# The feed-forward of a two-layer decoder trunk, cut into parts of 4, 6, 6 and 6 hidden chunks instead of 6, 8 and 8

## The chip, the core and the metric

The kernel runs on one core of one Trainium2 chip. A core has a matrix engine (TensorE, PE in the profile, with its weight loads shown as PEld), a vector engine (VectorE, DVE), an activation engine (ScalarE, ACT), a general engine (GpSimd, POOL) and a sync engine (SyncE, SP) that here issues nearly all DMAs from HBM. The metric is the device time of one execution in microseconds (us); lower is better. Three executions of the kernel before took 1247.47, 1247.70 and 1248.56 us, so its median is 1247.7 us.

## The reference

The input is a sequence of 512 tokens with 1024 features in float32. Two layers follow each other: the first mixes tokens with a causal convolution module, the second with differential attention. Behind each mixer come a SwiGLU feed-forward and a gated per-layer embedding. The change touches the feed-forward alone:

```python
def swiglu(x, w_gate, w_up, w_down):
    return (jax.nn.silu(x @ w_gate) * (x @ w_up)) @ w_down

        u = rms_norm(h, ffn_norm_g[i])
        h = h + swiglu(u, ffn_w_gate[i], ffn_w_up[i], ffn_w_down[i])
        gate = jax.nn.sigmoid(rms_norm(h, ple_norm_g[i]) @ ple_w_gate[i])
        h = h + gate * (p[i] @ ple_w_proj[i])
```

The hidden width is 2816, which is 22 chunks of 128 rows.

## The kernel before

Everything is held transposed: features on the 128 partitions, the 512 tokens along the free dimension. The stream `h` is eight tiles of 128x512. Each float32 operand of a matmul is split into two parts in the format float32r: `hi` is a cast on ScalarE, `lo` is the operand less `hi`, a subtraction on VectorE. A product then takes three matmuls (`mm3`, lines 166 to 168: lo x hi, hi x hi, hi x lo). Weights are split on the chip as they arrive: `weight` (lines 147 to 162) loads a 128x1024 tile into one of two buffers `wraw` from the SP queue (line 155), casts it (line 159) and subtracts (line 161) into one of four buffers `whi` and `wlo`.

The feed-forward (`ffn`) runs through the hidden chunks in parts, given by `PARTS` as (first chunk, number of chunks): 6, 8 and 8. A part makes its hidden chunks, and then `linear` projects them down and adds the result into `h` (line 881), eight outputs one after the other, the first two together (`group0` is 2). In the last part the new `h` also goes to the next norm.

The chunks of the first part are plain. Gate and up each take 8 x 3 matmuls of 512 columns, lines 869 to 875 scale with the norm's factor `rb`, apply SiLU, multiply, and split the hidden chunk into tiles B0, B1 and so on. `rb` is there only after the first chunk's matmuls. While these chunks run, `Operands.chunk` (lines 664 to 688), called four times behind the plain chunks that `OPS_AT` names, makes the operands of the products that follow.

The chunks of the later parts go in pairs. For a pair, the gate (and the same for up) is a 2x2 block product, done with seven products instead of eight: a `Unit` needs sums of weight blocks (S1 to S4), sums of activation blocks (T1 to T4, from `Operands`), and seven products of 4 x 3 matmuls with 256 columns each. `Unit.load` fetches two weight tiles (line 703; for a gate into A0 and A1, for an up into `wraw`). `Unit.prep` has six steps: 0 splits the blocks A11 and A12, 1 makes S1 and S2 on GpSimd (lines 720 and 721), 2 splits them (for the first unit of a part into four `wk` tiles, lines 726 and 727), 3 makes S3 and S4 on GpSimd (lines 732 and 733), 4 splits S3 (lines 736 and 737), 5 splits S4 and A22. The splits that go through `two` stand at lines 710 and 711. A run over the units of a part prepares each unit while the one before multiplies; the products 4 and 3 of a unit are placed behind the products 1 and 2 of the next one, and those of the last unit stand at the run's end.

The first unit of a part has no unit ahead of it. `HOOKS` places its load and its steps in the projection of the part before: the load at output 5, steps 1 and 3 at output 6, steps 0, 2, 4 and 5 at output 7. This is the order in which the program is written. The order in which each engine and each queue gets its instructions is set by a planner, which simulates the program and puts what is ready first, unless an edge says otherwise: `tc.issue_after(ins)` queues what its block writes for the engine of `ins` behind `ins`. It orders issue on that one engine and waits for nothing.

Of the kernel before, what the change touches and what calls it, by code (L numbers as in the profile page):

```python
# [15 lines left out]
ALU = mybir.AluOpType  # L16
# [7 lines left out]
NC = D // P  # L24
# [2 lines left out]
KW = 31  # L27
DFF = 2816
FC = DFF // P
PARTS = [(0, 6), (6, 8), (14, 8)]  # L30
EPS = 1e-6
LAMBDA_INIT = 0.8 - 0.6 * math.exp(-0.3 * 1)
NEG = -1.0e30
# [44 lines left out]
LT = 2  # L78
LA = 4
PACK = True  # L80
OPS_AT = (1, 2, 4, 5)
HOOKS = {5: (None,), 6: (1, 3), 7: (0, 2, 4, 5)}
HT = S // 2
E1 = True
GLO = 1
QKV = (("q", 0, (0, 0, 0, 0)), ("v", 0, (1, 1, 1, 2)), ("q", 1, (1, 1, 1, 2)), ("q", 2, (1, 1, 2, 1)), ("v", 1, (1, 1, 2, 2)), ("q", 3, (1, 1, 1, 1)))

PROJ1 = 16 + 2 + 8 + 2 * FC + 3 * NC + 8 + 4 * len(QKV)


@with_exitstack
def trunk(ctx, tc, xT, pT, wts, diag, dww, vec, rel, onehot, lamv, out):
# [9 lines left out]
    def sb(shape, tag, bufs, dt=F32):  # L102
        uid[0] += 1
        return pool.tile(shape, dt, tag=tag, name=f"{tag}_{uid[0]}", bufs=bufs)
# [10 lines left out]
    f = lambda ap: ap.bitcast(F32)  # L115
# [27 lines left out]

    wnext = [0]
    loaded = [None]

    def weight(n=1024, pieces=1, between=(), eng=V, after=(None, None), home=None, parts=None, bufs=1):
        i = wnext[0]
        wnext[0] += 1
        raw = sb([P, 1024], *(home or ("wraw", 2)))  # L150
        hi = sb([P, 1024], *((parts[0], bufs) if parts else ("whi", 4)), F32R)
        lo = sb([P, 1024], *((parts[1], bufs) if parts else ("wlo", 4)), F32R)
        for k in range(pieces):
            cut = slice(k * n // pieces, (k + 1) * n // pieces)
            loaded[0] = nc.sync.dma_start(raw[:, cut], wts[i, :, cut])
            if k < len(between):
                between[k]()
            with tc.issue_after(after[1].ins) if after[1] else nullcontext():
                A.copy(hi[:, cut], raw[:, cut])  # L159
            with tc.issue_after(after[0].ins) if after[0] else nullcontext():  # L160
                eng.tensor_tensor(lo[:, cut], raw[:, cut], f(hi[:, cut]), ALU.subtract)  # L161
        return hi, lo

    def mm3(acc, a, b, first, last, **kw):
        (ah, al), (bh, bl) = a, b
        T.matmul(acc, al, bh, start=first, stop=False, **kw)  # L166
        T.matmul(acc, ah, bh, start=False, stop=False, **kw)  # L167
        return T.matmul(acc, ah, bl, start=False, stop=last, **kw)  # L168
# [15 lines left out]
    def wpart(w, k):  # L184
        return tuple(
            t[k // 4][:, (k % 4) * P : (k % 4 + 1) * P] if isinstance(t, list) else t[:, k * P : (k + 1) * P] for t in w
        )
# [99 lines left out]
    def load(c):  # L287
        return lambda: nc.sync.dma_start(h[c], xT[c])

    w0 = weight(pieces=2, between=(load(0),))  # L290
    norm.split(0)
    w1 = weight(pieces=2, between=(load(1), load(2)))
    pair_loads = [loaded[0]]
    pairs = [(w1, w0)]
# [302 lines left out]
    with tc.manual_schedule(engines={V.engine, A.engine}):  # L597
        for c in range(NC + 2):
            if c < NC:
# [3 lines left out]
                hi = A.copy(z[c][0], y[c])  # L603
            if c >= 2:
                lo = V.tensor_tensor(z[c - 2][1], y[c - 2], f(z[c - 2][0]), ALU.subtract)
# [5 lines left out]
    def linear(n_in, src, consume, group0=1, before=None, after=None, split={}, home=None, given={}, at={}):  # L611


        m = 0
        while m < NC:
            g = group0 if m == 0 else 1
            ws = [
                given[m + i] if m + i in given
                else weight(n_in * P, after=split.get(m + i, (None, None)), home=home if m + i == 2 else None)
                for i in range(g)  # L620
            ]
            if m in at:
                at[m]()
            accs = [mm() for _ in range(g)]
            for k in range(n_in):
                if before:
                    before(k)
                for w_, a_ in zip(ws, accs):
                    mm3(a_, wpart(w_, k), src[k], k == 0, k == n_in - 1)
                    if after:  # L630
                        after()
            for i in range(g):
                consume(m + i, accs[i])
            m += g
# [170 lines left out]
    def ffn(norm, after, spare):  # L805
        rb = None
        ops = Operands(norm, spare)

        def units(n, hid):
            us = []  # L810
            for i in range(0, n, 2):
                g, u = Gate(2 * (i // 2), i == 0, "A"), Up(2 * (i // 2) + 1, False, "wraw")
                g.hid = hid
                u.gate, u.at, u.hid = g, i, hid
                us += [g, u]
            for x in us:
                x.b = ops.at
            return us

        def run(us):  # L820
            for n, x in enumerate(us):
                last = us[n - 1] if n else None
                nxt = us[n + 1] if n + 1 < len(us) else None
                x.start()
                if nxt:
                    nxt.load()
                x.p(1)
                if nxt:
                    nxt.prep(0)
                x.p(2)  # L830
                if nxt:
                    nxt.prep(1)
                if last:
                    last.p(4)
                x.p(6)
                if nxt:
                    nxt.prep(2)
                if last:
                    last.p(3)
                x.p(5)  # L840
                if nxt:
                    nxt.prep(3)
                    nxt.prep(4)
                x.p(7)
                if nxt:
                    nxt.prep(5)
            us[-1].p(4)
            us[-1].p(3)

        us = None  # L850
        for at, (f0, n) in enumerate(PARTS):
            if us:
                run(us)
                hid = us[0].hid
            else:
                hid = []
            for i in range(0 if us else n):
                wg, wu = weight(), weight()
                pg, pu = mm(), mm()
                for k in range(NC):  # L860
                    mm3(pg, wpart(wg, k), norm.u[k], k == 0, k == NC - 1)
                if rb is None:
                    norm.diagonal()
                for k in range(NC):
                    mm3(pu, wpart(wu, k), norm.u[k], k == 0, k == NC - 1)
                if rb is None:
                    rb = norm.rows()
                tg, tu = big(), big()
                V.tensor_tensor(tg, pg, rb, ALU.mult)
                A.activation(tg, tg, AF.Silu)  # L870
                V.tensor_tensor(tu, pu, rb, ALU.mult)
                V.tensor_tensor(tu, tu, tg, ALU.mult)
                hl = sb([P, 2, S], f"B{i}", 1, F32R)
                A.copy(hl[:, 0], tu)
                V.tensor_tensor(hl[:, 1], tu, f(hl[:, 0]), ALU.subtract)
                hid.append((hl[:, 0], hl[:, 1]))
                if i in OPS_AT:
                    ops.chunk(OPS_AT.index(i), rb)

            def add(m, acc):  # L880
                V.tensor_tensor(h[m], acc, h[m], ALU.add)
                if at == len(PARTS) - 1:
                    after.chunk(m)

            hooks = {}
            if at < len(PARTS) - 1:
                n2 = PARTS[at + 1][1]
                now = wnext[0]
                wnext[0] += NC
                us = units(n2, [None] * n2)  # L890
                end = wnext[0]
                wnext[0] = now
                x = us[0]
                for m, steps in HOOKS.items():
                    hooks[m] = partial(lambda steps: [x.load() if k is None else x.prep(k) for k in steps], steps)
            linear(n, hid, add, 2, at=hooks)
            if hooks:
                wnext[0] = end
# [281 lines left out]
    for what, at, pace in QKV:  # L1180
        ws = slab(GLO if at > 0 else 0)
        for tb in range(4):
# [12 lines left out]
            elif (what, at, tb) == ("q", 0, 2):  # L1195
                n = wnext[0]
                wnext[0] = PROJ1
                pw = [weight(parts=("B6", "B7"))]
# [6 lines left out]
            elif (what, at, tb) == ("q", 2, 1):  # L1205
                pw.append(weight_in_h(PROJ1 + 1, 0))
            elif (what, at, tb) == ("q", 2, 2):
                w_o1 = weight_in_h(PROJ1 + 3, 4)
            elif (what, at, tb) == ("q", 3, 1):
                wnext[0] = PROJ1 + 2  # L1210
                w_o0 = weight(parts=("B0", "B1"))
                wnext[0] = PROJ1 + 4
    unit_end(*waiting)


    done, steps = [0], [0]
# [82 lines left out]
def _layout(a):  # L1299
# [12 lines left out]
    def ffn(i):  # L1312
        g, u = _stationary(a["ffn_w_gate"][i]), _stationary(a["ffn_w_up"][i])
        r = []
        for f0, n in PARTS:
            plain = n if f0 == 0 else 0
# [84 lines left out]
```

## Time and profile before

| | |
|---|---|
| median of the runs | 1247.7 us |
| the profiled execution | 1246.62 us |
| its span, from the first to the last instruction | 1244.5 us |
| feed-forward of layer 0, from the norm's factor to the last projection's end (218.87 to 549.18) | 330.3 us |
| busy share of PE, DVE, ACT, POOL | 99%, 70%, 50%, 38% |
| clock granted to TensorE | 0.999 |

The profile shows one execution. Its page gives the busy time of each engine, the span in 40 slices, the chain of work that ended last, and groups of instructions by line with the idle time in front of them and what ended it. Other answers give the busy time by stage, the instructions in order of time, and the waits. A row of the timeline reads: start, duration, engine, line, operation, output tile and input tiles, shape, and in brackets the idle time before it with its releaser. A row of stages reads: window, its length, and for each engine the busy time and the number of instructions, then the granted clock, the DMA engines' share and GB/s. Tiles are named by their tags: `wraw`, `whi`, `wlo` are weights, A0 to A7 hold the normed stream in the plain part and weight sums later, B tiles hold hidden chunks, C, D, `wth`, `wtl` and `bias` hold activation operands, `mm` is PSUM.

### The profile page before, as it was taken

How to read it: one execution, taken by the hardware profiler on the slowest of the kernel's cores; microseconds unless marked ns; L12 is line 12 of the kernel's file. 1: busy time of each engine (PE TensorE's matmuls, PEld its weight loads, DVE VectorE, ACT ScalarE, POOL GpSimd, SP SyncE). 2: the span in 40 equal slices, each digit the busy share in tenths (PEclk: the TensorE clock that was granted, in tenths of full speed). 3: DMA queues.
4: the chain of work that ended last, by engine and by line, in shares of the span. 5: the costliest groups of instructions: out<-in, count | busy, mean ns of one | idle time of the engine just before them, and what ended most of it. 6: DMA issues, size and time to landing. Idle time of an engine off the chain costs nothing.

```text
span 1244.5 us, 18421 instructions
## 1 busy us (share of the span) xinstructions
PE 1234.6 (99%) x7080; PEld 1081.8 (87%) x7080; DVE 877.2 (70%) x1230; ACT 623.7 (50%) x1096; POOL 469.7 (38%) x355
## 2 busy tenths in 40 slices
PE   9999999999999999999999999999999999999998
PEld 8888788888998899888888888788889998999887
DVE  6997865975895478547676876647966885588535
ACT  6652454533553255434566877735434552455432
POOL 3863432024670464132336635141026640562220
PEclk9999999999999999999999999999999999999999
DMA  7566224224323332334432330152232333232331
GB/s 267 185 213 195 77 57 121 90 100 125 96 92 119 102 94 77 102 104 152 124 114 80 104 100 29 52 153 85 90 127 90 102 114 109 83 102 87 104 98 67
DMA packets 49154, 136.33 MB, mean 110 GB/s; under 512 B 5635, under 2 KB 10243, under 8 KB 49068
## 3 DMA queue, kind: packets, MB, share of 16 engines
q1 hardware_dynamic: 46944, 131.74, 34.0%
q10 hardware_dynamic: 2124, 3.43, 0.9%
q8 instruction: 55, 0.90, 0.3%
q14 instruction: 31, 0.25, 0.1%
HBM read 128.84 MB, written 6.31 MB: 109 GB/s over the span
## 4 chain that ended last, share of the span: by engine, by line
PE 96%; DVE 2%; issue 1%; ACT 0%; POOL 0%; DVEq 0%; ACTq 0%; POOLq 0%
PE mm L166 29%; PE mm L167 29%; PE mm L168 29%; PE sc L398 2%; PE mm L1117 1%; PE tp L199 1%; PE sc L1085 1%; PE sc L1084 1%; PE tp L1104 1%; PE mm L398 1%; PE tp L1038 1%; PE mm L354 1%; DVE wlo L711 0%; PE tp L282 0%; PE tp L141 0%
## 5 line engine op out<-in xcount | busy, mean ns | idle before, releaser
L159 ACT CAST whi<-wraw 128x1024 fp32r<-128x1024 f32 (+2 forms) x145 | 145.6, 1013 | 218.3 <-PE mm L168 96.7
L161 DVE TENSOR_TENSOR wlo<-wraw,whi 128x1024 fp32r<-128x1024 f32 (+2 forms) x141 | 179.2, 1277 | 69.4 <-ACT whi L159 69.1
L166 PE MATMUL mm<-A,wlo 128*128 128x512 f32 (+1 forms) x568 | 222.1, 391 | 0.1
L167 PE MATMUL mm<-A,whi 128*128 128x512 f32 (+1 forms) x568 | 219.5, 387 | 0.0
L168 PE MATMUL mm<-A,whi 128*128 128x512 f32 (+1 forms) x568 | 217.3, 389 | 0.0
L166 PE MATMUL mm<-B,wlo 128*128 128x512 f32 x352 | 137.0, 389 | 0.0
L167 PE MATMUL mm<-B,whi 128*128 128x512 f32 x352 | 137.0, 389 | 0.0
L168 PE MATMUL mm<-B,whi 128*128 128x512 f32 x352 | 135.6, 389 | 0.0
L229 POOL TENSOR_TENSOR acc<-acc,wk 128x512 f32<-128x512 f32 x35 | 58.4, 1670 | 193.4 <-ACT wk L228 192.9
L166 PEld LDWEIGHTS mm<-A,wlo 128*128 128x128 f32 x568 | 106.8, 188 | 23.1 <-issue 1.4
L167 PE MATMUL mm<-C,whi 128*128 128x256 f32 x448 | 126.8, 283 | 0.0
L168 PE MATMUL mm<-C,whi 128*128 128x256 f32 x448 | 126.8, 283 | 0.0
L166 PE MATMUL mm<-C,wlo 128*128 128x256 f32 x448 | 126.8, 283 | 0.0
L167 PEld LDWEIGHTS mm<-A,whi 128*128 128x128 f32 x568 | 106.9, 188 | 22.0 <-issue 1.0
L168 PEld LDWEIGHTS mm<-A,whi 128*128 128x128 f32 x568 | 106.5, 188 | 22.0 <-issue 0.5
L711 DVE TENSOR_TENSOR wlo<-A,whi 128x1024 fp32r<-128x1024 f32 x60 | 105.7, 1769 | 19.1 <-ACT whi L710 19.1
L710 ACT CAST whi<-A 128x1024 fp32r<-128x1024 f32 x60 | 62.9, 1048 | 54.5 <-PE mm L168 43.3
L720 POOL TENSOR_TENSOR A<-wraw 128x512 f32<-128x512 f32 x16 | 22.5, 1408 | 170.4 <-DMA wraw<-in_wts 156.1
L720 POOL TENSOR_TENSOR A<-A 128x512 f32<-128x512 f32 x16 | 25.2, 1575 | 162.3 <-DMA A<-in_wts 162.3
L167 PEld LDWEIGHTS mm<-C,whi 128*128 128x128 f32 x448 | 86.0, 192 | 0.2
L166 PEld LDWEIGHTS mm<-C,wlo 128*128 128x128 f32 x448 | 86.0, 192 | 0.2
L168 PEld LDWEIGHTS mm<-C,whi 128*128 128x128 f32 x448 | 86.0, 192 | 0.0
(309 smaller groups left out, 3031.2 us busy)
## 6 DMA issues: line engine op xcount, KB each, us to landing
wraw<-in_wts SPq DMA_DIRECT2D x161, 512.0 KB, 3.6
A<-in_wts SPq DMA_DIRECT2D x32, 512.0 KB, 3.6
wraw<-in_wts SPq DMA_DIRECT2D x16, 384.0 KB, 3.1
D<-in_diag SPq DMA_DIRECT2D x22, 256.0 KB, 4.6
C<-in_diag SPq DMA_DIRECT2D x16, 256.0 KB, 5.1
h<-in_xT SPq DMA_DIRECT2D x8, 256.0 KB, 5.3
rest<-h SPq DMA_DIRECT2D x8, 256.0 KB, 2.4
bias<-scr ACTq DMA_DIRECT2D x8, 256.0 KB, 3.6
```

The lines of the kernel that those rows point to most:

```text
L159: A.copy(hi[:, cut], raw[:, cut])
L161: eng.tensor_tensor(lo[:, cut], raw[:, cut], f(hi[:, cut]), ALU.subtract)
L166: T.matmul(acc, al, bh, start=first, stop=False, **kw)
L167: T.matmul(acc, ah, bh, start=False, stop=False, **kw)
L168: return T.matmul(acc, ah, bl, start=False, stop=last, **kw)
L199: r = T.matmul(t[:, cut], src[:, cut], ones, start=first and b == 0, stop=last and b == 3)
L229: self.last = self.eng.tensor_tensor(self.acc, self.acc, sq, ALU.add)
L354: last_tap[0] = T.matmul(acc, dg[:, j % 4], ups[c][:, j : j + S], start=(j == 0), stop=(j == PE_TAPS[c] - 1))
L398: last_tap[0] = T.matmul(acc[:, g * P : (g + 1) * P], w, ups[c][:, g, LEAD - m : LEAD - m + P], start=(m == 0), stop=(m == LAGS - 1),)
L710: A.copy(hi, src)
L711: V.tensor_tensor(lo, src, f(hi), ALU.subtract)
L720: G.tensor_tensor(s[:, 0], r1[:, 0], r1[:, 1], ALU.add)
```

## The change

There are four parts in each layer in place of three: 4 plain chunks, and then three parts of 6 chunks in seven-product pairs. So two chunks of each layer go from plain to seven-product, and there is one more projection. `OPS_AT` moves the four calls of `Operands.chunk` behind the plain chunks 0 to 3. The load of a part's first unit gets an edge that queues it on SP behind the last weight load that the program had written before it (that of output 5), and the steps get an edge that queues their VectorE instructions behind the last weight's subtraction written before them (that of output 6 or 7). Their ScalarE and GpSimd instructions get no edge. The weights on HBM are laid out in the new order.

```diff
-PARTS = [(0, 6), (6, 8), (14, 8)]
+PARTS = [(0, 4), (4, 6), (10, 6), (16, 6)]
...
-OPS_AT = (1, 2, 4, 5)
+OPS_AT = (0, 1, 2, 3)
 HOOKS = {5: (None,), 6: (1, 3), 7: (0, 2, 4, 5)}
...
-PROJ1 = 16 + 2 + 8 + 2 * FC + 3 * NC + 8 + 4 * len(QKV)
+PROJ1 = 16 + 2 + 8 + 2 * FC + len(PARTS) * NC + 8 + 4 * len(QKV)
...
+    split = [None]
...
-                eng.tensor_tensor(lo[:, cut], raw[:, cut], f(hi[:, cut]), ALU.subtract)
+                split[0] = eng.tensor_tensor(lo[:, cut], raw[:, cut], f(hi[:, cut]), ALU.subtract)
...
                 x = us[0]
+
+                def ahead(steps):
+                    for k in steps:
+                        if k is None:
+                            with tc.issue_after(loaded[0].ins):
+                                x.load()
+                        else:
+                            with tc.issue_after(split[0].ins):
+                                x.prep(k)
+
                 for m, steps in HOOKS.items():
-                    hooks[m] = partial(lambda steps: [x.load() if k is None else x.prep(k) for k in steps], steps)
+                    hooks[m] = partial(ahead, steps)
```

## The prediction

> **What bounds the kernel now.** I read the page first (busy time, clock, the chain that ended last), then the busy time by stage, then the waits and the timeline around the hand-overs between stages.
>
> ```profile
> span 1244.5 us, 18421 instructions
> PE 1234.6 (99%) x7080; PEld 1081.8 (87%) x7080; DVE 877.2 (70%) x1230; ACT 623.7 (50%) x1096; POOL 469.7 (38%) x355
> PEclk9999999999999999999999999999999999999999
> PE 96%; DVE 2%; issue 1%; ACT 0%; POOL 0%; DVEq 0%; ACTq 0%; POOLq 0%
> ```
>
> PE is busy in 99% of the span, at the full granted clock, and 96% of the chain is PE. So time is won in two ways only: fewer or shorter matmul steps, or one of the few moments in which PE waits. A busy time of one matmul (283 ns for 256 columns) overlaps its neighbour; what counts is the step from one start to the next. I take it from stages with a known number of matmuls. The rows below are the four runs of seven-product units (the answer is for line 168, one of the three lines of each product, 216 of them in a run and one that was still ending: 648 matmuls in all), and a projection of six chunks (8 outputs x 6 x 3 = 144 matmuls).
>
> ```profile
> core 0: us, PE busy (x) PEld busy (x), PEclk, DMA share, GB/s
> 300.38:378.54 78.16, 61.12 (x217) 41.47 (x216) 1.00 0.32 97
> 424.98:502.74 77.76, 61.13 (x217) 41.47 (x216) 1.00 0.29 83
> 945.03:1023.54 78.51, 61.12 (x217) 41.45 (x216) 1.00 0.32 96
> 1069.99:1147.80 77.81, 61.12 (x217) 41.46 (x216) 1.00 0.27 83
> ...
> core 0: us, PE busy (x) PEld busy (x) DVE busy (x) ACT busy (x) POOL busy (x), PEclk, DMA share, GB/s
> ...
> 267.74:300.38 32.64, 32.64 (x146) 27.04 (x144) 21.89 (x22) 10.19 (x13) 12.30 (x8) 1.00 0.36 112
> ```
>
> 77.76/648 = 0.1200 us for a matmul of 256 columns; 32.64/144 = 0.2267 us for one of 512. Half the columns cost 53%, not 50%. And the first run of each layer (78.16, 78.51) is longer than the second (77.76, 77.81) by 0.40 and 0.70 us: these are waits.
>
> **The change: fewer matmul steps.** A plain chunk has gate and up, 8 x 3 matmuls each: 48 x 0.2267 = 10.88 us. A pair of seven-product chunks has two units of 7 x 4 x 3 = 84: 168 x 0.1200 = 20.16 us. Each layer turns two plain chunks (21.76) into one pair (20.16): 1.60 us less. Down projections keep 22 chunks x 8 x 3 matmuls however they are cut. Two layers: -3.2 us.
>
> The Trainium skill, in "TensorE: Matmul & The Clock Gate", section "Wait — 56ns, not 53.3ns?", gives a warm step of N/2.4 GHz plus 2.5 ns, an estimate of 109 and 216 ns here; with it the two layers would save 4.7 us. The trace has 120 and 226.7 ns for the same steps and decides.
>
> **The first turn behind the projection's weights.** What do the first runs wait for that the second ones don't?
>
> ```profile
> 355.91 5.05 SPq L703 DMA_DIRECT2D A<-in_wts  x2
> 365.28 34.21 SPq L155 DMA_DIRECT2D wraw<-in_wts  x8
> 364.26 2.12 POOL L720 TENSOR_TENSOR A<-A 128x512 f32<-128x512 f32 x1 [0.79 <-DMA A<-in_wts]
> 369.88 2.16 POOL L733 TENSOR_TENSOR A<-A,A 128x512 f32<-128x512 f32 x1
> 368.57 2.32 DVE L711 TENSOR_TENSOR wlo<-A,whi 128x1024 fp32r<-128x1024 f32 x1
> 375.48 1.23 DVE L161 TENSOR_TENSOR wlo<-wraw,whi 128x1024 fp32r<-128x1024 f32 x1 [0.49 <-ACT whi L159]
> 1018.44 0.28 PE L168 MATMUL mm<-C,whi 128*128 128x256 f32 x1
> 1019.12 0.39 PE L166 MATMUL mm<-wth,wlo 128*128 128x256 f32 x1 [0.40 <-DVE big L768]
> ```
>
> Only a part that another follows has hooks. Before its first down weight (365.28) SP loads the next part's first turn (355.91), POOL makes its four sums (364.26 to 372.04), and a split of 1024 columns beside them takes 2.32 us, where one after them takes 1.23. So VectorE's read of an accumulator (L768) is late and PE waits, here 0.68 us between two starts. With the change the load stands on SP behind the sixth down weight, and VectorE's splits behind the eighth; POOL's sums aren't ordered but need the load. They leave the run's end, and these waits go: -1.1 us (0.40 + 0.70), bounded by 0 and 1.2.
>
> Durations for the parts below:
>
> ```profile
> A<-in_wts SPq DMA_DIRECT2D x32, 512.0 KB, 3.6
> L711 DVE TENSOR_TENSOR wlo<-A,whi 128x1024 fp32r<-128x1024 f32 x60 | 105.7, 1769 | 19.1 <-ACT whi L710 19.1
> L161 DVE TENSOR_TENSOR wlo<-wraw,whi 128x1024 fp32r<-128x1024 f32 x121 | 159.2, 1321 | 64.1 <-ACT whi L159 63.8
> L161 DVE TENSOR_TENSOR wlo<-wraw,whi 128x768 fp32r<-128x768 f32 x16 | 17.3, 1090 | 4.5 <-ACT whi L159 4.5
> L710 ACT CAST whi<-A 128x1024 fp32r<-128x1024 f32 x60 | 62.9, 1048 | 54.5 <-PE mm L168 43.3 <-issue 10.1 <-ACT big L783 0.3
> L869 DVE TENSOR_TENSOR big<-mm,rb 128x512 f32<-128x512 f32 x12 | 8.3, 688 | 9.7 <-ACT rb L257 6.9 <-PE mm L168 2.7
> L875 DVE TENSOR_TENSOR B<-big,B 128x512 fp32r<-128x512 f32 x12 | 10.4, 868 | 0.0
> L881 DVE TENSOR_TENSOR h<-mm,h 128x512 f32<-128x512 f32 x48 | 32.8, 687 | 66.4 <-PE mm L168 66.4
> ```
>
> **One part more.** Each layer gets eight more weight loads, casts, splits and sums into h, at equal bytes (the same 2816 rows of weight). A sum is 0.69 us of VectorE, eight are 5.5 us beside more than 30 us of PE, and the loads are shorter: nothing on the path.
>
> **Run ends.** There are three in each layer where there were two. The last unit's products 4 and 3 have no next unit to hide behind; the projection's first two outputs stand in, and after them the last hidden chunk is still to be made.
>
> ```profile
> 378.54 0.40 PE L166 MATMUL mm<-B,wlo 128*128 128x512 f32 x1
> 383.32 0.28 PE L166 MATMUL mm<-C,wlo 128*128 128x256 f32 x1
> 386.20 0.40 PE L166 MATMUL mm<-B,wlo 128*128 128x512 f32 x1
> 381.51 1.22 DVE L161 TENSOR_TENSOR wlo<-wraw,whi 128x1024 fp32r<-128x1024 f32 x1 [2.37 <-ACT whi L159]
> 387.74 1.22 DVE L161 TENSOR_TENSOR wlo<-wraw,whi 128x1024 fp32r<-128x1024 f32 x1
> 386.68 0.41 DVE L773 TENSOR_TENSOR wk<-wk,mm 128x256 f32<-128x256 f32 x1
> 388.87 0.69 DVE L802 TENSOR_TENSOR B<-wk,B 128x512 fp32r<-128x512 f32 x1
> 395.49 1.37 DVE L881 TENSOR_TENSOR h<-mm,h 128x512 f32<-128x512 f32 x2 [5.14 <-PE mm L168]
> ```
>
> From 378.54 to 383.32 PE does 21 matmuls of the projection, then the 24 of products 4 and 3, and at 389.56 the last hidden chunk is there, 3.36 us after 386.20. A part of eight has 6 x 2 x 3 = 36 matmuls that don't need the last pair, so 15 (3.40 us) are left for that gap: covered. A part of six has 24, so 3 (0.68 us) are left. The third output's 12 (2.72 us) can fill the rest, once L773 has freed its accumulator at 387.09, 0.2 us after PE gets there. Bounds: 0, and 3.36 - 0.68 = 2.7 us if nothing fills. I take 0.2, because the third output's weight was split by 382.7 in the old order, shorter weights come no later, and it stood in there already: the first sums into h come at 395.49, 41 matmuls after 386.20, and the first two outputs had only 27 left. Six ends: +1.2 us.
>
> **The first turn, later.** With its load behind the weights, is it late in its turn? The load of two tiles takes at most 2 x 3.6 us, POOL 7.8, then casts and splits of up to 1.05 + 1.77 us (rows above): some 18 us behind the sixth load. In a projection of six chunks (32.6 us) that is covered: two buffers take the weights in turn, so the sixth load can leave when the fourth weight is split, at 388.96 in the old order (L161 at 387.74), 2.8 us after the last unit's last matmul; PE has 30 us of projection behind that. In the new one of four chunks (8 x 12 x 0.2267 = 21.76 us) the first products need only A11 and A12, which need no sum; S2 is needed 24 x 0.12 = 2.9 us into the run, S4 and A22 after 10 us. Queued behind these loads on SP are the seventh and eighth weight, about 7 us later than else; six outputs of 2.72 us stand ahead of the seventh. I take 0; if that cover is gone, at most PE waits the 7 us once in each layer.
>
> **VectorE's cover at the layer's start.** The operands of the seven products (four chunks of VectorE work) are now made within four plain chunks instead of six. From the row in which the norm's factor is there to the first run:
>
> ```profile
> 218.87:300.38 81.51, 81.51 (x362) 67.48 (x360) 63.80 (x88) 32.78 (x45) 12.30 (x8) 1.00 0.34 104
> ...
> 226.00:262.00 36.00, 36.00 (x160) 29.82 (x159) 33.13 (x53) 16.31 (x23) 0.00 (x0) 1.00 0.30 89
> ```
>
> PE's 81.5 us lose two plain chunks (21.8) and a third of the projection (48 matmuls, 10.9): 48.9 us stay. VectorE's 63.8 lose two chunks' work (2 x 1.32 for splits, about 4 x 0.75 for the hidden chunk: 5.7 each) and a third of eight splits (8 x 0.36): 49.5 stay. That is more than there is room for. Some 6 us can fall into the run without harm (S1, S2, S3, S4/A22 and the last two sums), which leaves 43.4 us for 48.9: VectorE must be 89% packed. Over the whole old stretch it was 78% (63.80/81.51), but then it had nothing to do for part of it; in the stretch where its queue was full (226 to 262) it was 92%. At 92% the cost is 0, at 78% it is 43.4/0.78 - 48.9 = 6.8 us in each layer. I take 0, since a full queue is the nearer row, and keep 6.8.
>
> The Trainium skill ("SBUF — State Buffer", section "Who interferes with whom") says that a VectorE instruction with two SBUF inputs and a GpSimd one that reads SBUF hold their common port in turn, each for its whole length. The trace agrees (2.32 against 1.23 us above); it speaks for the packing below 92% where POOL's sums run, and so for the second rival.
>
> **The sum.** The profiled execution took 1246.6 us, 1.1 under the median of 1247.7. 1246.6 - 3.2 - 1.1 + 1.2 = 1243.5; with 1.1 back, 1244.7.
>
> **Rivals.**
> 1. *The gain is given back at hand-overs.* 0.7 us at each of the six run ends, or VectorE 85% packed at the layer starts (2.2 us each), cancel the 4.3 us. For it: the stretch is nearly full. Against: PE waited 1.2 us at all hand-overs of before together. Time about 1247.7.
> 2. *VectorE becomes the bound at the layer's start* (slower). At 78% both layers lose 13.6 us: 1247.7 - 4.3 + 13.6 + 1.2 = 1258. It decides from 83% down, where the loss passes 3.4 us in each layer. For it: 17.7 us of idle shrink to none. Against: most of that idle was lack of work.
> 3. *The last hidden chunk isn't covered at run ends* (slower): 6 x 2.7 = 16 us, 1247.7 - 4.3 + 16.2 = 1259.6, deciding from 1.1 us each. Against: the 14 matmuls of a third output that stood in before.
> 4. *The added narrow matmuls cost half a wide one*, 0.1133 us: 168 x 0.1133 = 19.0, so 5.4 saved: 1247.7 - 5.4 - 1.1 + 1.2 = 1242.4. Against it is each of the four runs. By the Trainium skill's formula above it would be 1243.1, and the same rows speak against that.
>
> **How the numbers follow.** Forecast 0.47, rival 1 0.27, rival 2 0.13, rival 3 0.11, rival 4 0.02. A measurement of this kernel tells about 0.2% (2.5 us) from no change: under 1245.2 is faster, over 1250.2 slower. The forecast's own range is 1243 to 1246.5; 0.43 of its 0.47 lie under 1245.2, and with rival 4 faster is 0.45. Same takes the rest of it and rival 1: 0.31. Slower is rivals 2 and 3: 0.24. The range 1242.5 to 1253 holds the forecast, rivals 1 and 4 and the milder forms of 2 and 3; some 0.15 lies above it.
>
> **What would show it.** Two runs' waits for L768 gone and runs of six at 60.5 us (504 matmuls x 0.12) show the first two steps. PE steps over 0.3 us behind a run's end would show rival 3; VectorE without idle and PE waiting for an L711 or L680-685 at the first unit would show rival 2. The prediction is wrong if such waits sum to over 2 us in a layer.

## The result and the profile after

The changed kernel takes 1265.76 us (median of four runs, 1265.55 to 1266.94), the kernel before 1247.59 beside it: a ratio of 1.0138 with a 95% interval of 1.0124 to 1.0152. It is 18 us slower where 3 us less was forecast, and it lies above the range. The profiled execution took 1266.94 us.

The page after begins like this (lines below here are the changed kernel's, one more than before from line 147 on):

```profile
span 1265.1 us, 18889 instructions
PE 1237.9 (98%) x7224; PEld 1087.6 (86%) x7224; DVE 887.9 (70%) x1278; ACT 639.8 (51%) x1138; POOL 494.0 (39%) x371
PEclk9999999999999999999999999999999999999999
PE 85%; DVE 5%; DMA 2%; issue 2%; POOL 1%; ACT 1%; SPq 1%; ACTq 0%; DVEq 0%; POOLq 0%
```

PE's share of the chain fell from 96% to 85%: a tenth of the path now runs through other engines. The waits of PE say where (what waited, for what, total us, times, longest):

```profile
PE mm L167 <- DVE wlo L162: 13.5, 6, 3.4
PE mm L167 <- ACT big L761: 1.9, 1, 1.9
```

Six times PE waits for the subtraction that makes `wlo`, the low part of a down weight. There was no such row before. The row that was there before, a wait for `big` of L768, is gone. The second row is new as well: it stands in the first run of the second layer.

The busy time by stage gives the price. First PE in the feed-forward of the two layers, from the matmul that makes the norm's factor to the same matmul of the embedding's norm behind it; before:

```profile
217.19:565.73 348.54, 348.39 (x2171) 1.00 0.33 101
861.85:1210.80 348.95, 348.55 (x2172) 1.00 0.33 100
```

and after:

```profile
218.77:579.57 360.80, 352.12 (x2244) 0.99 0.32 98
875.74:1230.95 355.21, 348.45 (x2243) 1.00 0.32 99
```

The layers are 12.3 and 6.3 us longer, 18.5 of the 20.6 us by which the spans differ. (Another 1.6 us lie ahead of the feed-forward. One of the experiments below keeps the old parts and starts it at 218.88 too, so I don't count them to the new parts.) Then single projections and runs of the changed kernel, with PE's busy time, the granted clock, the DMA share and GB/s:

```profile
247.56:274.53 26.97, 23.55 (x98) 0.94 0.44 133
274.53:332.13 57.60, 57.60 (x482) 1.00 0.28 82
339.79:372.24 32.45, 29.56 (x125) 0.95 0.42 134
437.49:469.69 32.20, 29.82 (x126) 0.95 0.44 135
534.94:562.98 28.04, 28.04 (x125) 1.00 0.33 99
904.53:929.10 24.57, 22.07 (x97) 1.00 0.36 121
929.10:989.11 60.01, 58.10 (x481) 1.00 0.29 90
996.77:1026.17 29.40, 28.20 (x125) 1.00 0.46 148
1091.43:1120.81 29.38, 28.24 (x126) 1.00 0.44 148
354.40:357.40 3.00, 2.98 (x7) 0.51 0.50 134
```

A run's 480 matmuls take 57.60 us, 0.1200 each: no wait. The last projection of a layer, which no part follows, has 28.04 us for the 123 matmuls behind the last unit. The same 123 take 32.45, 32.20, 29.40 and 29.38 us where another part follows: 4.4, 4.2, 1.4 and 1.3 lost. The first projections, 96 x 0.2267 = 21.76 us, take 26.97 and 24.57: 5.2 and 2.8 lost. The first run of the second layer loses 2.4 of its 60.01. Together 21.7 us. With the 3.2 and 1.1 us won that is +17.4; the 28.04 us themselves hold 0.16 above 123 x 0.2267, which is 1.0 if it is taken for all six run ends. So the 18.5 us are accounted for.

What happens at such a hand-over? The projection behind the first run, in order of time on SP, GpSimd, ScalarE, VectorE and PE (start, duration, engine, line; in brackets the idle time and its releaser), and from the view of the A tiles the time from the load's issue to its landing:

```profile
341.88 0.33 SPq L156 DMA_DIRECT2D wraw<-in_wts  x1
342.26 0.90 SPq L704 DMA_DIRECT2D A<-in_wts  x2
DMA to landing us min/median/max: 6.2/6.6/6.9
349.81 1.29 POOL L721 TENSOR_TENSOR A<-A 128x512 f32<-128x512 f32 x1 [33.05 <-DVE h L882]
351.13 0.62 ACT L727 CAST wk<-A 128x512 fp32r<-128x512 f32 x1 [8.02 <-POOL A L721]
351.65 1.56 ACT L160 CAST whi<-wraw 128x768 fp32r<-128x768 f32 x2
349.08 1.37 DVE L882 TENSOR_TENSOR h<-mm,h 128x512 f32<-128x512 f32 x2 [5.24 <-PE mm L169]
352.51 1.85 DVE L162 TENSOR_TENSOR wlo<-wraw,whi 128x768 fp32r<-128x768 f32 x1 [2.06 <-ACT whi L160]
354.42 0.79 PE L167 MATMUL mm<-B,wlo 128*128 128x512 f32 x1 [2.89 <-DVE wlo L162]
355.01 0.63 PE L168 MATMUL mm<-B,whi 128*128 128x512 f32 x1
355.44 0.63 PE L169 MATMUL mm<-B,whi 128*128 128x512 f32 x1
```

Read it from the end. PE waits 2.89 us for a split that VectorE starts at 352.51, because ScalarE's cast of that weight runs only at 351.65. (The split itself takes 1.85 us beside GpSimd's sums; the one at 358.41, with no sum beside it, takes 0.96.) ScalarE had been idle for 8.02 us. What stood at the head of its queue was L727, the cast of S1 of the *next part's first turn*, and that waited for GpSimd's sum, which waited for the load of 342.26, 6 to 7 us under way. (The row names L882 as GpSimd's releaser, but GpSimd's sum doesn't read `h`. The landing, 342.3 to 342.7 plus 6.2 to 6.9, fits 349.81 as well, and at the second projection of the layer, where the same happens, the trace names the load: L721 at 446.98 follows an idle time ended by `A<-in_wts`, and ScalarE had been idle for 7.48 us.) Two weights were cast together behind it, so they had been ready.

The 2.4 us of the second layer's first run are of the same kind, one turn later. PE stops at 933.29 for a copy on ScalarE (L761, at 935.01). Ahead of the copy stood the casts of the next unit's sums (L737 at 932.82, after 5.04 us of idle time ended by GpSimd's sum), and GpSimd had waited until 928.21 for that unit's load into `wraw`.

In the first projections something else is in the way (ScalarE, then VectorE, the same kernel):

```profile
257.62 0.62 ACT L727 CAST wk<-A 128x512 fp32r<-128x512 f32 x1 [2.74 <-POOL A L721]
258.14 1.13 ACT L160 CAST whi<-wraw 128x512 fp32r<-128x512 f32 x2
257.95 2.48 DVE L882 TENSOR_TENSOR h<-mm,h 128x512 f32<-128x512 f32 x4 [1.82 <-PE mm L169]
260.36 2.20 DVE L162 TENSOR_TENSOR wlo<-wraw,whi 128x512 fp32r<-128x512 f32 x2
```

Four sums into `h` stand together: four outputs end at the same moment. Until then they hold all four buffers of `whi` and `wlo`, so the fifth weight can't be split, and then the four sums stand ahead of its subtraction. (L727 stands ahead of the casts here too; the experiments separate the two.)

### The profile page after: what moved, and what is told of

It reads as the page before. It is cut to its first block, busy times and chain, and to the rows that moved or that the text cites. A ratio compares the mean times of both kernels' runs of the same rounds, so it can differ in the third digit from the quotient of the medians.

```text
span 1265.1 us, 18889 instructions
## 1 busy us (share of the span) xinstructions
PE 1237.9 (98%) x7224; PEld 1087.6 (86%) x7224; DVE 887.9 (70%) x1278; ACT 639.8 (51%) x1138; POOL 494.0 (39%) x371
## 4 chain that ended last, share of the span: by engine, by line
PE 85%; DVE 5%; DMA 2%; issue 2%; POOL 1%; ACT 1%; SPq 1%; ACTq 0%; DVEq 0%; POOLq 0%
PE mm L167 26%; PE mm L168 26%; PE mm L169 26%; DVE wlo L162 2%; PE mm L1128 1%; DVE sc L450 1%; DMA A<-in_wts 1%; PE sc L1096 1%; PE sc L1095 1%; PE tp L1115 1%; PE sc L399 1%; PE mm L399 1%; PE tp L1049 1%; PE mm L355 1%; PE tp L200 0%
## 5 line engine op out<-in xcount | busy, mean ns | idle before, releaser
L167 PE MATMUL mm<-A,wlo 128*128 128x512 f32 (+1 forms) x504 | 197.1, 391 | 1.1 <-ACT A L207 1.0
L168 PE MATMUL mm<-A,whi 128*128 128x512 f32 (+1 forms) x504 | 194.4, 387 | 0.0
L169 PE MATMUL mm<-A,whi 128*128 128x512 f32 (+1 forms) x504 | 192.5, 389 | 0.0
L169 PE MATMUL mm<-C,whi 128*128 128x256 f32 x492 | 139.2, 283 | 0.0
L168 PE MATMUL mm<-C,whi 128*128 128x256 f32 x492 | 139.2, 283 | 0.0
L167 PE MATMUL mm<-C,wlo 128*128 128x256 f32 x492 | 139.2, 283 | 0.0
L721 POOL TENSOR_TENSOR A<-A 128x512 f32<-128x512 f32 x18 | 30.8, 1709 | 241.2 <-DMA A<-in_wts 205.1
L167 PEld LDWEIGHTS mm<-A,wlo 128*128 128x128 f32 x504 | 94.8, 188 | 22.1 <-ACT A L207 1.5
L169 PEld LDWEIGHTS mm<-A,whi 128*128 128x128 f32 x504 | 94.5, 188 | 19.9 <-issue 0.5
L168 PEld LDWEIGHTS mm<-A,whi 128*128 128x128 f32 x504 | 94.7, 188 | 19.5 <-issue 1.0
L711 ACT CAST whi<-A 128x1024 fp32r<-128x1024 f32 x66 | 69.1, 1049 | 52.1 <-issue 24.4
L168 PEld LDWEIGHTS mm<-C,whi 128*128 128x128 f32 x492 | 94.4, 192 | 0.2
L167 PEld LDWEIGHTS mm<-C,wlo 128*128 128x128 f32 x492 | 94.4, 192 | 0.2
L169 PEld LDWEIGHTS mm<-C,whi 128*128 128x128 f32 x492 | 94.4, 192 | 0.0
L167 PEld LDWEIGHTS mm<-B,wlo 128*128 128x128 f32 x352 | 67.3, 191 | 30.1 <-DVE wlo L162 16.6
```

The costliest lines, as they stand in the source:

```text
L711: A.copy(hi, src)
L721: G.tensor_tensor(s[:, 0], r1[:, 0], r1[:, 1], ALU.add)
```

## The experiments

Two causes were put to the test. *The queue cause*: the first turn's load and its ScalarE and GpSimd work, queued late and without an edge on ScalarE, make the weights of a six-chunk projection late. *The buffer cause*: in a projection of four chunks the planner lets outputs 3 and 4 fill the time until the last hidden chunk is there, all four weight buffers stay taken, and the fifth weight is late. The rival to both is that VectorE is simply too full. The table gives the feed-forward of each layer in each profile, as in the windows above; the old parts have 348.54 and 348.95 us.

| kernel | layer 0, us | layer 1, us | time, us | ratio to before, interval |
|---|---|---|---|---|
| changed kernel | 360.80 | 355.21 | 1265.76 | 1.0138, 1.0124 to 1.0152 |
| new parts without edges | 355.81 | 355.73 | 1261.41 | 1.0107, 1.0092 to 1.0122 |
| old parts with the edges | 348.13 | 348.12 | 1246.98 | 0.9993, 0.9984 to 1.0002 |
| load's edge alone | 361.77 | 356.56 | 1269.87 | 1.0172, 1.0151 to 1.0192 |
| load one output earlier | 356.26 | 357.43 | 1264.00 | 1.0130, 1.0113 to 1.0146 |
| ScalarE edge added | 352.99 | 354.96 | 1259.74 | 1.0091, 1.0073 to 1.0110 |
| that, parts 6, 6, 6, 4 | 354.41 | 353.99 | 1257.03 | 1.0067, 1.0050 to 1.0084 |
| ScalarE edge, first outputs in order | 350.19 | 351.27 | 1251.29 | 1.0021, 1.0011 to 1.0030 |
| ScalarE edge, two more weight tiles | 349.97 | 348.92 | 1249.20 | 1.0007, 0.9997 to 1.0016 |
| two more tiles, no edges | 352.19 | 350.88 | 1254.41 | 1.0052, 1.0038 to 1.0066 |
| two more tiles, no load edge | 352.55 | 352.01 | 1255.94 | 1.0070, 1.0057 to 1.0083 |
| two more tiles, hooks one later | 355.41 | 355.68 | 1261.05 | 1.0105, 1.0091 to 1.0118 |
| two more tiles, load edge in the first projection alone | 348.21 | 347.93 | 1247.18 | 0.9996, 0.9987 to 1.0006 |

"Lost" below is the time from one matmul's start to the next less its step (0.227 or 0.120 us), added up at one place.

**The parts without the edges, and the edges without the parts.**

```diff
-                            with tc.issue_after(loaded[0].ins):
-                                x.load()
+                            x.load()
...
-                            with tc.issue_after(split[0].ins):
-                                x.prep(k)
+                            x.prep(k)
```

> The new parts alone, without the two edges. Theory A: the first turn is loaded early, nothing waits for it on ScalarE in the projections; what is left is 3.2 us fewer matmul steps and the waits for L768-like reads at run ends that the first turn's sums make, now in two runs of each layer: 1244 to 1249 us. Theory B: the waits in the first projection of each layer stay, 1252 to 1257 us. If the six waits come from the shorter outputs of the new parts and not from the edges, 1262 us or more.

```diff
-PARTS = [(0, 4), (4, 6), (10, 6), (16, 6)]
+PARTS = [(0, 6), (6, 8), (14, 8)]
...
-OPS_AT = (0, 1, 2, 3)
+OPS_AT = (1, 2, 4, 5)
```

> The two edges alone, on the old parts of 6, 8 and 8. Theory A: with outputs of 4.1 and 5.4 us the planner puts the cast of the sum behind the sixth weight's cast, and the seventh weight is needed later; the waits for L768 at the first run's end go: 1245.5 to 1248 us. If a late first turn costs a wait in each projection whatever the parts: four projections at some 3.5 us, 1258 us or more.

The waits of PE in the first of the two:

```profile
PE mm L167 <- DVE wlo L162: 7.4, 2, 3.7
PE mm L169 <- DVE B L876: 2.5, 2, 1.6
```

The new parts alone cost 13.8 us, all of it in the two first projections (8.7 and 8.6 lost): two waits for a weight, two for the last hidden chunk's split. No six-chunk projection loses anything. The edges alone cost nothing: with the old parts both layers run with PE busy all the time, 0.4 and 0.8 us shorter, which is the wait for L768 gone; in the time that can't be told from no change. So the six-chunk losses need both the parts and the edges, and the first projections' need the parts only. The old parts came out in the range expected of them; the new parts alone show the waits of theory B, but above its 1252 to 1257 us.

**Which edge, and which queue.** First the load's edge without those of the steps; then both edges of the changed kernel, with the load one output earlier; then the ScalarE instructions of the steps queued behind the weight's cast as well.

```diff
-                            with tc.issue_after(split[0].ins):
-                                x.prep(k)
+                            x.prep(k)
```

> The new parts with the load's edge alone (no edge on the splits). Theory A: the late load is what holds ScalarE, so the waits of 4 us in the projections of six chunks stay as in the changed kernel: 1263 to 1267 us. If the edge on VectorE's splits makes them: none there, 1260 to 1262 us as with no edge at all.

```diff
-HOOKS = {5: (None,), 6: (1, 3), 7: (0, 2, 4, 5)}
+HOOKS = {4: (None,), 6: (1, 3), 7: (0, 2, 4, 5)}
```

> The changed kernel with the first turn's load one output earlier (behind the fifth down weight's load, not the sixth's), no other edge. The load leaves some 5 to 9 us earlier, so it has landed when ScalarE reaches the cast of the sum. Theory A: the waits go though the order on ScalarE keeps the cast of the sum ahead of the fifth weight's: 1243 to 1248 us. Theory B: 1254 to 1256 us. Theory C: the two tiles now stand ahead of one weight more, 1264 us or more.

```diff
+    cast = [None]
...
-                A.copy(hi[:, cut], raw[:, cut])
+                cast[0] = A.copy(hi[:, cut], raw[:, cut])
...
-                            with tc.issue_after(split[0].ins):
+                            with tc.issue_after(split[0].ins), tc.issue_after(cast[0].ins):
```

> The changed kernel, with one edge more: the ScalarE casts of a part's first turn are queued behind the last down weight's cast as well. Theory A (in the changed kernel the cast of the first turn's sum, L727, stands on ScalarE ahead of the casts of the fifth and sixth down weight and holds them while its load lands): all six waits of PE in the projections go, 1243 to 1246 us. Theory B (VectorE lacks cover at the layer's start): the waits in the first projection of each layer stay, about 10 us in all, 1254 to 1256 us. Theory C (the seventh and eighth down weight come late because the first turn's two tiles stand ahead of them on SP): nothing changes, 1264 to 1266 us.

The load's edge alone makes the six-chunk losses: 4.3, 4.0, 2.0 and 1.8 us, as theory A had it, though the time is 3 us above its range, since the first projections rise to 6.6 and 5.4 as well. Loaded one output earlier they are 0.6, 0.8, 1.7 and 0.8, but the first projections rise to 7.3 and 6.7: in layer 0 the early turn's L727 now stands on ScalarE ahead of the cast of the last hidden chunk (253.26, after 4.66 us of idle time), and that chunk's subtraction takes 1.85 us beside the sums. So the 1264.00 us lie where theory C expected them, but it isn't SP's order that holds PE up there. With the ScalarE edge the six-chunk losses of layer 0 are gone and those of layer 1 fall only from some 1.4 to 1.2 each; 6 us are won. In layer 1 the first run's 2.4 us fall to 0.3, but its first projection rises from 2.8 to 5.4, so that the layer as a whole gains only 0.25 us. PE's wait for weights in that profile, and ScalarE and VectorE in its first projection:

```profile
PE mm L168 <- DVE wlo L163: 8.6, 4, 3.5
254.50 0.68 DVE L877 TENSOR_TENSOR B<-big,B 128x512 fp32r<-128x512 f32 x1
260.19 1.14 ACT L161 CAST whi<-wraw 128x512 fp32r<-128x512 f32 x2 [3.13 <-PE mm L170]
260.15 2.48 DVE L883 TENSOR_TENSOR h<-mm,h 128x512 f32<-128x512 f32 x4 [1.83 <-PE mm L170]
262.55 2.05 DVE L163 TENSOR_TENSOR wlo<-wraw,whi 128x512 fp32r<-128x512 f32 x2
```

The time fits none of the three ranges: some of the waits went, as in theory A, and some stayed, as in theory B. The queue cause is shown for the six-chunk projections of layer 0, and the first projections stand at 5.1 and 5.4. In that of layer 0 the last hidden chunk was split at 255.2, five microseconds before the four outputs end at 260.1; ScalarE and VectorE both sat idle (3.13 and 1.83) until PE had ended these outputs, and then the sums went ahead of the split. That fits the buffer cause and speaks against a full VectorE.

What is left in the six-chunk projections of layer 1 can be read in the same profile. Here is the fifth weight's split with GpSimd's sum beside it, first in layer 1, then in layer 0:

```profile
1002.45 2.05 DVE L163 TENSOR_TENSOR wlo<-wraw,whi 128x768 fp32r<-128x768 f32 x1
1002.40 1.29 POOL L723 TENSOR_TENSOR A<-A,A 128x512 f32<-128x512 f32 x1
352.53 0.95 DVE L163 TENSOR_TENSOR wlo<-wraw,whi 128x768 fp32r<-128x768 f32 x1
352.59 2.04 POOL L734 TENSOR_TENSOR A<-A,A 128x512 f32<-128x512 f32 x1
```

In layer 1 the sum started 0.05 us before the split, and the split took 2.05 us. In layer 0 the split started first and took 0.95, and the sum took 2.04. What PE loses between two starts in layer 1, 1.10 us, is the 1.10 by which the split was longer. The second six-chunk projections show the same pair (1.99 and 0.95). So the moved sums cost PE time a second way: they now run beside the weights' splits.

**Is it the buffers?** A fifth pair of buffers was not tried. In a part of four chunks the hidden chunks' tiles B4 and B5 are free, and a weight of 4 x 128 columns fits one of them with both its parts. This version puts the fifth and sixth weight there, with the ScalarE edge:

```diff
+        if both_in:
+            hi, lo = both(sb([P, 2, S], both_in, 1, F32R))
...
-                else weight(n_in * P, after=split.get(m + i, (None, None)), home=home if m + i == 2 else None)
+                else weight(n_in * P, after=split.get(m + i, (None, None)), home=home if m + i == 2 else None,
+                            both_in=f"B{m + i}" if n_in == 4 and m + i in (4, 5) else None)
```

> The kernel with the ScalarE edge (1259.7 us), and in the first projection of each layer the fifth and sixth down weight are split into tiles B4 and B5, which are free then, so that they need none of the four weight buffers. PE's written order stays. Theory D (PE fills the wait for the last hidden chunk with the third and fourth output; all four weight buffers are then held until the four outputs end together, and the fifth weight can only be made after that): the waits of 5.1 and 5.4 us in the first projections fall to about 1 us each, which is the sum into h that frees an accumulator: 1250 to 1253 us. Theory B (VectorE has too much to do there): unchanged, 1258 to 1261 us.

The first projections lose 0.38 us each (about 1 was expected, and the time is 0.8 us under its range), 10.5 us are won, and the waits of PE for a weight shrink to one row, 1.7 us in all. They stand in the six-chunk projections of layer 0, which lose 1.1 us each, again behind a split beside GpSimd's sums (1.97 us at 346.07):

```profile
PE mm L171 <- DVE wlo L166: 1.7, 2, 0.9
```

Two other ways to break the same knot: outputs of the first projection in order, and a four-chunk part at the layer's end, where no first turn follows.

```diff
-                    mm3(a_, wpart(w_, k), src[k], k == 0, k == n_in - 1)
+                    with tc.issue_after(done_first.ins) if done_first and n_in == 4 else nullcontext():
+                        last_mm = mm3(a_, wpart(w_, k), src[k], k == 0, k == n_in - 1)
...
+            done_first = last_mm
```

> The kernel with the ScalarE edge, and in the first projection of each layer an edge on PE that queues each output's matmuls behind the output before, so nothing fills the wait for the last hidden chunk. Theory D: PE waits for that chunk once, 0.5 to 1.5 us, and then not for weights: 1251 to 1254 us. Theory B: VectorE's lateness is only met elsewhere, waits of 4 us or more stay in each first projection, 1257 us or more.

```diff
-PARTS = [(0, 4), (4, 6), (10, 6), (16, 6)]
+PARTS = [(0, 6), (6, 6), (12, 6), (18, 4)]
...
-OPS_AT = (0, 1, 2, 3)
+OPS_AT = (1, 2, 4, 5)
```

> Parts of 6 plain, 6, 6 and 4 with all edges: as many plain and seven-product chunks as before, one projection more, and the first projection with 6 chunks again. Theory D: no wait in the first projections, since they have 30 matmuls of their own before the last hidden chunk; at most 1.2 us in each later one: 1246.5 to 1250 us. If one part more costs what the changed kernel lost: 1257 us or more.

In order, the wait for the fifth weight is gone too, and the time is in the expected range. PE then waits where the fill had covered it, 0.6 us for the last hidden chunk, and afterwards for the first unit's own split (1.4 and 3.6 us lost):

```profile
PE mm L168 <- DVE wlo L716: 3.0, 2, 1.8
```

With the four-chunk part last, the first projections lose nothing and the last ones 5.8 and 3.7 us, so the time missed its range by 7 us. The wait follows the four chunks; VectorE makes the next norm there as well, so this run alone doesn't say that it is the buffers again.

**What the load's edge is good for.** With the tiles B4 and B5: no edges at all; all edges but the load's; all three, with the first turn one output later; and the load's edge in the first projection alone.

> The new parts without any edge, and the fifth and sixth weight of each layer's first projection in the free tiles B4 and B5. Theory D (the four weight buffers, all held to the end of four outputs, make the first projections wait, and the edges make the other projections wait): the waits of 8.7 and 8.6 us of the cut alone fall to under 1 us each, no projection of six chunks waits, and the time is 1261.4 less about 16, 1244 to 1246.5, under the kernel before by 0.1 to 0.3%. Rival C (the cut alone waits because the first turn's own work, unordered, is in VectorE's way in the first projection, not because of buffers): at least 3 us stay in each first projection and the time is 1250 or more. Rival P (the new parts cost 2 to 4 us somewhere that is no wait in a projection): 1247 to 1249.

> The ScalarE and VectorE edges and the free tiles B4 and B5 as before, but the first turn's load has no edge, so SP may fetch it ahead of the last weights. Theory A (a late load makes the waits of the six-chunk projections): the waits of 1.13, 1.07 and 0.3 us there go, and the time falls from 1249.2 to 1246 to 1247.5. Rival S (the two edges on the splits and casts make them): they stay within 0.3 us of what they were, 1248.5 to 1249.5.

```diff
-HOOKS = {5: (None,), 6: (1, 3), 7: (0, 2, 4, 5)}
+HOOKS = {6: (None,), 7: (1, 3, 0, 2, 4, 5)}
```

> All three edges and the free tiles B4 and B5, with the first turn's load behind the sixth output's weight load instead of the fifth's, and its steps behind the seventh's split. Theory A (the later the first turn stands behind weights, the later the seventh or eighth weight): waits of 1 us or more move to the last output's weight or the run's first unit, 1249 to 1254. Rival S (sums on GpSimd beside the seventh weight's split are the price): later sums leave that split alone, the six-chunk waits fall under 0.3 us, 1246.5 to 1248.5.

```diff
-                            with tc.issue_after(loaded[0].ins):
+                            with tc.issue_after(loaded[0].ins) if n == 4 else nullcontext():
```

> The free tiles B4 and B5 and the ScalarE and VectorE edges, and the load's edge in the projection of the four plain chunks alone. Theory (in that projection the load's edge keeps GpSimd's sums out of VectorE's way while it is behind; in the projections of six chunks, where VectorE has room, the same edge only makes the weights late): first projections wait 0.4 us each as with all edges, six-chunk projections not at all as without the load's edge, and the time is 1249.2 less 2.5, 1246 to 1247.5. Rival (the two kinds of projection aren't independent, what the load gives in one the next run takes back): some wait of 1 us or more appears, 1248 to 1251.

My expectation for the first of these was missed by 8 us, and it is its rival that came true: without edges 5.0 and 3.0 us stay in the first projections. Without the load's edge alone they lose 5.5 and 5.0, while the six-chunk ones lose nothing: that half of the second expectation was met, its time was not. VectorE and GpSimd in that profile, what PE then waits for, and the same two VectorE instructions with the load's edge:

```profile
249.13 1.79 DVE L166 TENSOR_TENSOR wlo<-wraw,whi 128x512 fp32r<-128x512 f32 x1
248.76 1.61 POOL L726 TENSOR_TENSOR A<-A 128x512 f32<-128x512 f32 x1 [35.75 <-DMA A<-in_wts]
253.85 1.62 POOL L739 TENSOR_TENSOR A<-A,A 128x512 f32<-128x512 f32 x1
256.95 0.68 DVE L881 TENSOR_TENSOR B<-big,B 128x512 fp32r<-128x512 f32 x1
PE mm L171 <- DVE h L887: 6.0, 2, 3.0
249.45 0.68 DVE L166 TENSOR_TENSOR wlo<-wraw,whi 128x512 fp32r<-128x512 f32 x1
252.87 0.68 DVE L881 TENSOR_TENSOR B<-big,B 128x512 fp32r<-128x512 f32 x1
```

GpSimd's sums of the first turn run from 248.76 to 255.5, in the middle of the plain part's last VectorE work, and a subtraction that takes 0.68 us alone takes 1.79 beside them. VectorE does the same work in the same order in both runs, and four of its instructions take 6.85 us in place of 2.46. The last hidden chunk is split at 256.95; with the load's edge it was 252.87. The sums into `h` (L887) come later still. So in the first projection the load's edge is needed: it keeps GpSimd away while VectorE is full. Queued one output later in every projection, the first turn is late for its run (3.0, 4.0, 4.2 and 2.8 us lost in the second and third runs of the two layers), the other end of the same scale, and 7 us dearer than expected. The six-chunk projections themselves then lose only 0.1 us each: the sums come after the split, which takes 0.95.

With the edge in the first projection only, the time is in the expected range: the first projections lose 0.4 us each and the six others 0.1 to 0.2. Three of the eight:

```profile
247.43:269.59 22.16, 22.05 (x97) 1.00 0.49 162
335.19:363.23 28.04, 28.04 (x125) 1.00 0.39 118
979.72:1007.76 28.04, 28.04 (x125) 1.00 0.38 117
```

The cut with nearly all its waits removed thus takes 1247.18 us beside 1247.39 before: not to be told from it. No version that was run beats the kernel before by more than can be measured.

## Why the prediction was wrong

**Fewer matmul steps, -3.2: right.** Runs of six chunks go at 0.1200 us a matmul (57.60/480), with no wait in five of six runs. But it is also the whole prize. In the last experiment a layer takes 348.21 and 347.93 us, the old parts with the edges 348.13 and 348.12: the 1.6 us a layer are spent on short waits: 0.38 us in the first projection, 0.34 in the run behind it, 0.11 at each of the three run ends, and smaller ones. By the sums they come to 1.7 us more than with the old parts in layer 0 and 1.4 in layer 1. That is rival 1, for the cut at its best.

**The first turn behind the weights, -1.1: right in its place.** The waits for L768 are gone, and the old parts with the edges show 0.4 and 0.8 us. But the sums that made them didn't vanish. They left the run's end and went beside the weights' splits of the projection, where a split of 0.95 us takes up to 2.05; I had asked only what they leave.

**"The first turn, later: I take 0" is the first step that failed.** I followed the load on SP and the subtractions on VectorE, and looked for lateness at the seventh weight and in the run's first turn. The load took no longer than I had priced (2 x 3.6 us; at the place shown it landed 6.2 to 6.9 us after its issue). I left out ScalarE, although the steps have no edge there. L727 stood in its queue ahead of the casts of the fifth and sixth weight, and ScalarE had 8.02 us with nothing to do. The cap, 7 us once in each layer, was the wrong shape as well: it was 4.4 + 4.2 us in layer 0 and 1.4 + 1.3 in layer 1, with 2.4 more in a run. The ScalarE edge took out layer 0's share. The 1.2 us that stay in layer 1 are the split beside GpSimd's sum; without the load's edge, when the sums run elsewhere, they are gone.

**"Run ends": right where it was worked out, and the second failed step where it wasn't.** The third output's matmuls do fill the gap. The two last projections of the changed kernel take 0.16 us more than their 123 matmuls, and so do, within 0.04, all six behind the runs of the last experiment: 1.0 us in all where I had put 1.2. No row of the changed kernel's waits is for a last hidden chunk. But I took the fill as free and never costed the end of the *plain* part, which shrank from six chunks to four. There outputs 3 and 4 fill, all four end together, and four buffers are given back at once: 5.2 and 2.8 us for which the sum has no term. Two more tiles for weights took 10.5 us out of the kernel that had 5.1 and 5.4 lost there. "One part more, nothing on the path" falls with it, since it is the shorter projection that runs out of buffers.

**VectorE's cover at the layer's start: right for a reason I had not given.** I asked for 89% and expected 92%. In the changed kernel it is 90%:

```profile
222.00:258.00 36.00, 36.00 (x161) 29.80 (x160) 32.54 (x57) 15.77 (x26) 1.70 (x2) 1.00 0.23 74
```

and PE has no wait in that stretch. But it holds because the load's edge leaves GpSimd 1.70 us of work there; I had reckoned with a full queue alone. In the version without it the subtractions slow to 1.79 us and PE does wait: rival 2's mechanism, held off by the edge whose price I had put at 0.

Rivals 2 and 3 had forecast 1258 and 1259.6, nearer than my number, but neither happened as told: in the changed kernel VectorE didn't bind, and the last hidden chunk was covered. That they came nearer is luck. (A slip: 1243.5 with 1.1 back is 1244.6, not 1244.7; nothing hangs on it.) The view that would have warned was in the trace of before: each projection of six chunks has 48 matmuls less than one of eight, 10.9 us less cover for everything that stands in a queue beside it, and I checked that cover for one queue at a time.

## What to carry to other kernels

An edge that holds back one engine's share of a step leaves the others' share where it was, and an instruction that waits there for a late load can hold the ready ones behind it, as L727 did: cost a moved load in each queue that its consumers use. Work that is moved away from one place runs beside something else: ask what it slows there. Work that fills a wait also holds buffers, and outputs that end together give them back together; count the buffers over the fill, not only the matmuls. And a cut into more parts pays its hand-overs as often as there are parts: here waits of 0.1 to 0.4 us were enough to use up a saving of 1.6 us a layer.

## What the runs showed of the chip

Some waits of PE cost more than their length. After the wait that ends at 354.42 the next matmuls of 512 columns start 0.43 us apart (355.01 to 355.44), not 0.227, until about 357.4, and the granted clock of that stretch is 0.51 (last row of the windows of the changed kernel). That adds some 1.5 us to a wait of 3. In the first projection the mean over the whole of it is 0.94. The Trainium skill, "TensorE: Matmul & The Clock Gate", section "Part 1: The HAM clock gate", says that an idle window of about 3.4 us, which runs freely, sets the clock to half, and its section "Wait — 56ns, not 53.3ns?" gives 426.7 ns for 512 columns then; the trace agrees with the half and the 0.43 us. The wait of 2.89 us that was followed by it is shorter than the window that the page names. So was one of 1.85 us in the version with outputs in order (0.51 in 921.50 to 925.00), while one of 2.50 us in the changed kernel was not followed by it (1.00 in 918 to 921). What decides is not shown here.

A VectorE subtraction of 128x512 takes 0.68 us alone and 1.79 beside GpSimd's sums, 2.6 times as long. The prediction's pair, 2.32 against 1.23 us for 1024 columns, was 1.9 times. Which of the two engines is slowed can turn on 0.05 us, as the two layers of the ScalarE-edge version show.
